# Values and z projected with tokens stationary, a running minimum in the softmax, and the forgetting mask as a matmul

## The chip, the cores and the metric

The kernel runs on one core of one Trainium2 chip. A core has five engines that run side by side: TensorE (PE, with its weight loads shown apart as PEld), VectorE (DVE), ScalarE (ACT), GpSimd (POOL) and SyncE (SP), which here only issues DMA transfers. The metric is device time in microseconds (us) of one execution.

## The reference

One decoder layer on x of 2048 tokens by 1024 channels: an RMS norm, one wide input projection, three causal attention branches that read it, a SiLU gate z on each branch, a branch projection with a sigmoid gate, an output projection, a residual and a last RMS norm. Cut to what matters here:

```python
h = rmsnorm(x, norm_g[l]);  proj = h @ w_in[l]
# diff (4 heads of 128): two softmaxes with a linear bias, pd = p0 - lam * p1, o = pd @ v
# fox  (8 heads of 64):  s = q.k * scale + c[q] - c[k];  s = where(causal, s, -inf);  p = softmax(s);  o = p @ v
# dil  (8 heads of 64):  three banded patterns, each with its row max m, denominator and numerator, merged by exp(m - mx)
y = branch_out * silu(z)
```

## The kernel before

All projections use numbers split in two float16 halves, a high and a low one, so a product takes three matmuls (high.high, high.low, low.high) for each of the 8 blocks of 128 input channels: 24 matmuls that accumulate in one PSUM bank. The normalised input lies transposed on chip, channels on partitions, as `xT[half][token quarter]`, each 128 x 8 x 512.

The work runs as 12 groups, four of each branch (g0 to g3 diff, g4 to g7 fox, g8 to g11 dil). Each group has 128 channels of q and k for two heads (u = 0, 1), 128 of v and 128 of z, and some of the 24 merge-gate projections ride along. `drive` emits a group's attention as jobs; between their steps, the `Filler` emits pieces of projection work (v, then the next group's q and k, z, gates) by a credit in estimated nanoseconds: each generator step yields its estimate, and `pump` runs steps until the credit is spent. The order that then stands on each engine is made by a scheduler from this program order, from the dependencies and from the number of buffers in each pool.

A q/k, v, z or gate unit (`mm_steps`, line 385) takes 512 tokens: the 128 x 128 weight block is stationary and 512 columns of `xT` stream past, so the result has channels on partitions. That suits q and k. Values and z must have tokens on partitions. So `fill_v` and `z_unit` evict the bank as two float16 halves (ACT line 544 or 572, DVE line 545 or 573) and send them through a DMA transpose on SP's queue (line 546 or 574); for z, POOL then adds the two transposed halves (line 575). Dil groups also write v to DRAM and read it back in strides (lines 549, 1038, 1040).

A softmax row block (`softmax_rows`, 128 queries) runs over its keys in chunks of 512: two matmuls make the scores (`scores`, lines 661 and 662, tile `s_g`), and one DVE instruction (line 696, `CUSTOM_DVE_ANT_0`) adds the bias, writes the sum to an `e` tile and takes the row maximum of the chunk, which a second small instruction, `DVE_READ_ACCUMULATOR2_ANT`, puts into a column of `pm`. In fox, the last chunk is read in two such instructions: the block on the diagonal takes its bias from `bl`, a copy of the bias that POOL has masked (line 964), the rest takes `R`. Then a reduction over the columns (line 703) and a multiplication by minus the score scale (line 704, or 706 for one column) give `nm`, and ACT takes exp(c * e + nm) (line 710). The dil jobs do the same by blocks (lines 1109, 1112, 1114, 1118). After that, `e` is split in two float16 halves (ACT 727, DVE 728), transposed by DMA into `eT` (line 736, tile pool of 6), and multiplied with v on PE (lines 718, 721, tile `po_g`). The `e` tiles are a pool of 5 and become free when their transposes have landed; the score banks are 3 and become free when line 696 or 1109 has read them.

Of the kernel before, what the change touches and what calls it, by code (L numbers as in the profile page):

```python
# [19 lines left out]
P = 128  # L20
# [136 lines left out]
def tile_hybrid_trunk(  # L157
# [27 lines left out]
    make_identity(nc, ident)  # L185

# [341 lines left out]

    def fill_v(gr):
        if gr["br"] == 2:  # L530
            gr["vd"] = dr.tile([S, 2, P], F16, tag="vd", name=f"vd_{gr['n']}", bufs=2)
        wt = w_need(("v", gr["g"]))
        for t4 in range(4):
            pd = dn_bank(f"pv_{gr['n']}_{t4}")
            prs = []
            for k in range(KC):
                wh, wl = wsl(wt, 0, k), wsl(wt, 1, k)
# [22 lines left out]
    def z_unit(gr, t4):  # L560
        wt = w_need(("z", gr["g"]))
        z = gr["z"]
        pd = dn_bank(f"pz_{gr['n']}_{t4}")
        prs = []
        for k in range(KC):
            wh, wl = wsl(wt, 0, k), wsl(wt, 1, k)
            prs += [(wh, xT[0][t4][:, k]), (wh, xT[1][t4][:, k]), (wl, xT[0][t4][:, k])]
        yield from mm_steps(pd, prs, 216, 6)
        hl = gs_tile(f"zs_{gr['n']}_{t4}").bitcast(F16)
        zt = gs_tile(f"zt_{gr['n']}_{t4}").bitcast(F16).rearrange("p (b c) -> p b c", b=8)  # L570
# [88 lines left out]
    def scores(gr, u, q2s, qsl, ps, ksl):  # L659
# [12 lines left out]
    def softmax_rows(gr, u, q2, qb, bias_of, diag, den_of, name):  # L672
        n = qb + 1
        nk = n * P
        nch = (n + 3) // 4
        qsl = slice(P * qb, P * qb + P)
        off = P * (qb % 4)
        pm = st1("pm", f"pm_{name}", 5)
        np_ = 0
        et = []  # L680
        for ch in range(nch):
            w = min(512, nk - 512 * ch)
            if ch % 2 == 0:
                et.append(e_tile(f"e_{name}_{ch // 2}", (P, 1280)))
                live[0] += 1
            ps = sc_bank(f"s_{name}_{ch}")
            scores(gr, u, q2[:, off:off + P], qsl, ps[:, :w], slice(512 * ch, 512 * ch + w))
            o = 256 + 512 * (ch % 2)
            segs = [(0, w, bias_of(512 * ch, w))]
            if diag is not None and ch == nch - 1:  # L690
                segs = [(w - P, P, diag)]
                if w > P:
                    segs.append((0, w - P, bias_of(512 * ch, w - P)))
            for a, sw, b in segs:
                with hp(H_TT):
                    rd = V.tensor_tensor_reduce(out=et[ch // 2][:, o + a:o + a + sw], in0=ps[:, a:a + sw], in1=b, scale=1.0, scalar=-3e38,  # L696
                                           op0=ALU.add, op1=ALU.max, accum_out=pm[:, np_:np_ + 1])
                np_ += 1
            reads.append(rd)
            yield  # L700
        nm = st1("nm", f"nm_{name}")
        if np_ > 1:
            V.tensor_reduce(nm, pm[:, :np_], axis=AX.X, op=ALU.max)
            V.tensor_mul(nm, nm, gr["nc"][u])  # L704
        else:
            V.tensor_mul(nm, pm[:, 0:1], gr["nc"][u])
# [66 lines left out]
    def jobs_diff(gr):  # L773
# [7 lines left out]
        def job(qb):  # L781
# [5 lines left out]
            def S_():  # L787
# [6 lines left out]
                for u in range(2):  # L794
                    et = yield from softmax_rows(
                        gr, u, q2[u], qb, lambda a, w: bias[:, S - P - P * qb + a:S - P - P * qb + a + w], None,
# [6 lines left out]
                V.tensor_mul(a, den[:, 0, 0:1], nlam)  # L803
                V.tensor_mul(a, a, rO[:, qb, 1:2])
# [142 lines left out]
    def jobs_fox(gr):  # L947
# [6 lines left out]
        def job(u, qb):  # L954
# [4 lines left out]
            def S_():  # L959
                R = gr["R"][u]  # L960
                if qb % 4 == 0:
                    q2[u] = make_q2(gr, u, qb // 4)
                bl = bl_tile(f"bl_{name}")
                G.affine_select(out=bl, in_=R[:, P * qb:P * qb + P], pattern=[[-1, P]], compare_op=ALU.is_ge, fill=NEG,
                                base=0, channel_multiplier=1)
                hold["e"] = yield from softmax_rows(
                    gr, u, q2[u], qb, lambda a, w: R[:, a:a + w], bl,
# [75 lines left out]
    def jobs_dil(gr):  # L1043
# [17 lines left out]
        def job(p, bs):  # L1061
# [11 lines left out]
            def S_():  # L1073
# [3 lines left out]
                for h in range(0, len(bs), 2):  # L1077
# [5 lines left out]
                    nm = st1("nm2", f"nm_{name}_{h}", 4, 8)  # L1083
                    for a, b in enumerate(bs[h:h + 2]):
# [15 lines left out]
                        for u in range(2):  # L1100
                            cut = p == 0 and w > P and j % 4 == 0
                            am = st1("amx", f"amx_{name}_{b}_{u}", 2) if cut else None
                            for c in range(1 + cut):
# [62 lines left out]
    def post_dil(gr):  # L1166
# [511 lines left out]
```

## Time and profile before

| | |
|---|---|
| median of 3 runs (lowest, highest) | 2784.61 us (2780.58, 2785.28) |
| the profiled execution's own time | 2802.34 us |
| its span, first to last instruction | 2800.6 us |
| PE / DVE / ACT / POOL busy | 2634.3 / 2088.7 / 1669.5 / 383.4 us |
| mean granted TensorE clock | 0.932 |

The profile is of one execution, and its own time is 17.7 us (0.6%) above the median of the three timed runs. The span leaves 1.7 us of its time outside. Busy times are sums over instructions; PE's are modelled at their ends, so that a chain of short gaps can hide in a busy PE. The groups follow each other in time: diff from about 100 to 900 us, fox to 1650 us, dil to 2400 us, and then the branch and output projections.

### The profile page before, as it was taken

Reading aid. Unit: us, or ns where it says so; the run is one execution under the profiler, and the core shown is the slowest. Engines: PE = TensorE matmul, PEld = TensorE weight load, DVE = VectorE, ACT = ScalarE, POOL = GpSimd, SP = SyncE. Lnnn points to the kernel's source line nnn. Section 1 sums busy time; section 2 is a strip of 40 time slices with the busy share of each in tenths; the row PEclk is TensorE's granted clock in tenths of the full one; section 3 lists DMA queues with packets and bytes.
Section 4 is the critical chain, followed back from the end, with each engine's and each line's share of the span. In section 5 each row is a group of like instructions: output and inputs, shape, how many; then the busy total and the mean of one; then the engine's idle time right before and its main releaser. Section 6 shows DMA issues by size and latency. Waiting matters only on the chain.

```text
span 2800.6 us, 48432 instructions
## 1 busy us (share of the span) xinstructions
PE 2634.3 (94%) x16264; PEld 1378.4 (49%) x16264; DVE 2088.7 (75%) x7120; ACT 1669.5 (60%) x3642; POOL 383.4 (14%) x565
## 2 busy tenths in 40 slices
PE   7999999999999999999999998998979887999998
PEld 4455445455455444454455444544545444444555
DVE  8687978977977868778778776667667665678855
ACT  6466666656566666666676656756758577435311
POOL 0000200200102102102111120132041310400000
PEclk9899999989999999999999999998989998999999
DMA  4345445444455787887886878679687799764222
GB/s 159 74 88 111 89 92 108 99 83 110 90 105 112 140 162 143 159 156 148 150 167 131 153 137 145 133 149 162 138 158 156 139 204 230 212 187 137 95 100 76
DMA packets 981834, 377.02 MB, mean 135 GB/s; under 512 B 842824, under 2 KB 939856, under 8 KB 980048
## 3 DMA queue, kind: packets, MB, share of 16 engines
q1 hardware_dynamic: 981584, 373.93, 63.3%
q8 instruction: 127, 2.08, 0.3%
q14 instruction: 123, 1.01, 0.1%
HBM read 118.14 MB, written 59.05 MB: 63 GB/s over the span
## 4 chain that ended last, share of the span: by engine, by line
PE 58%; DVE 13%; DMA 12%; ACT 8%; issue 5%; SPq 2%; POOL 1%; DVEq 0%; ACTq 0%; POOLq 0%
PE pq_g L385 12%; PE pg L385 11%; PE pbr L385 9%; DMA eT_g<-e_g 6%; PE pz_g L385 5%; PE pout L1485 4%; PE po_g L718 3%; PE pv_g L385 3%; PE s_g L661 3%; PE s_g L662 3%; ACT e_g L1118 2%; DVE e_g L728 2%; PE pout L1486 2%; DVE e_g L696 2%; PE po_g L721 2%
## 5 line engine op out<-in xcount | busy, mean ns | idle before, releaser
L385 PE MATMUL pg<-xT,w_g 128*128 128x512 f16 x2304 | 582.9, 394 | 4.4 <-ACT gs L593 2.8
L710 ACT ACTIVATE e_g<-e_g,nm_g,c_g 128x1024 f32<-128x1024 f32 (+7 forms) x384 | 377.6, 984 | 251.4 <-DVE nm_g L704 218.4
L385 PE MATMUL pq_g<-xT,w_q 128*128 128x512 f16 x1536 | 388.4, 399 | 15.5 <-DVE stk_g L416 14.8
L728 DVE SCALAR_TENSOR_TENSOR e_g<-e_g 128x512 f16<-128x512 f32 (+2 forms) x480 | 316.4, 669 | 89.0 <-ACT e_g L727 86.4
L718 PE MATMUL po_g<-v_g,eT_g 128*128 128x128 f16 (+1 forms) x2232 | 315.4, 236 | 34.6 <-DMA eT_g<-e_g 16.8
L385 PEld LDWEIGHTS <-w_g 128*128 128x128 f16 x2304 | 223.6, 101 | 244.3 <-issue 13.9
L727 ACT ACTIVATE e_g<-e_g 128x512 f16<-128x512 f32 (+2 forms) x480 | 265.9, 569 | 91.3 <-DVE e_g L728 86.7
L385 PE MATMUL pz_g<-xT,w_z 128*128 128x512 f16 x1152 | 288.4, 390 | 6.5 <-DVE stk_g L416 5.3
L721 PE MATMUL po_g<-v_g,eT_g 128*128 128x64 f16 (+1 forms) x2232 | 293.6, 201 | 0.0
L385 PE MATMUL pv_g<-xT,w_v 128*128 128x512 f16 x1152 | 283.2, 395 | 2.8 <-DVE vs_g L545 1.4
L1118 ACT ACTIVATE e_g<-e_g,nm_g,c_g 128x256 f32<-128x256 f32 (+1 forms) x384 | 207.8, 543 | 111.0 <-DVE nm_g L1114 109.0
L385 PE MATMUL pbr<-u,w_b 128*128 128x512 f16 x1152 | 264.9, 393 | 4.1 <-ACT gs L593 1.9
L718 PEld LDWEIGHTS <-eT_g 128*128 128x128 f16 x2232 | 211.2, 100 | 87.0 <-DMA eT_g<-e_g 25.2
L661 PE MATMUL s_g<-stk_g 128*128 128x512 f16 (+3 forms) x640 | 228.1, 358 | 25.1 <-DVE pm_g L696 24.7
L721 PEld LDWEIGHTS <-eT_g 128*128 128x128 f16 x2232 | 206.5, 99 | 78.7 <-issue 21.7
L385 PEld LDWEIGHTS <-w_q 128*128 128x128 f16 x1536 | 148.7, 102 | 178.1 <-DVE stk_g L416 16.7
L696 DVE CUSTOM_DVE_ANT_0 e_g<-s_g,bias_g 128x512 f32<-128x512 f32 (+3 forms) x320 | 190.3, 605 | 60.8 <-DMA eT_g<-e_g 39.1
L662 PE MATMUL s_g<-stk_g,q_g 128*128 128x512 f16 (+3 forms) x640 | 229.0, 360 | 0.2 <-issue 0.2
L696 DVE CUSTOM_DVE_ANT_0 e_g<-s_g,R_g 128x512 f32<-128x512 f32 (+3 forms) x288 | 171.5, 597 | 43.9 <-DMA eT_g<-e_g 29.7
L385 PEld LDWEIGHTS <-w_b 128*128 128x128 f16 x1152 | 115.3, 100 | 146.6 <-issue 8.1
L385 PEld LDWEIGHTS <-w_v 128*128 128x128 f16 x1152 | 114.8, 101 | 134.9 <-issue 7.9
L1485 PE MATMUL pout<-wo,acc 128*128 128x512 f16 x512 | 172.7, 389 | 0.0
(476 smaller groups left out, 4331.7 us busy)
## 6 DMA issues: line engine op xcount, KB each, us to landing
gd<-gs SPq DMA_DIRECT2D x96, 256.0 KB, 2.7
gt<-gd SPq DMA_DIRECT2D x24, 1024.0 KB, 5.2
w_g<-in_w_in_dram SPq DMA_DIRECT2D x24, 512.0 KB, 4.1
ud<-y_g SPq DMA_DIRECT2D x48, 256.0 KB, 3.1
eT_g<-e_g SPq DMA_TRANSPOSE x640, 3.2
od_g<-ro_g SPq DMA_DIRECT2D x64, 132.0 KB, 2.3
xb<-in_x_dram SPq DMA_DIRECT2D x16, 512.0 KB, 6.5
q_g<-stk_g SPq DMA_DIRECT2D x128, 64.0 KB, 2.3
```

Source lines behind the costliest of these rows:

```text
L385: T.matmul(dst, l, r, start=(i == 0), stop=(i == n - 1))
L661: behind_read(T.matmul(ps, stk[:, 0, qsl], stk[:, 1, ksl], start=True, stop=False))
L662: T.matmul(ps, q2s, stk[:, 1, ksl], start=False, stop=True)
L696: rd = V.tensor_tensor_reduce(out=et[ch // 2][:, o + a:o + a + sw], in0=ps[:, a:a + sw], in1=b, scale=1.0, scalar=-3e38, op0=ALU.add, op1= ...
L710: A.activation(e[:, 256:256 + w], e[:, 256:256 + w], AF.Exp, bias=nm, scale=gr["c"][u], accum_out=den_of(i))
L718: ins = T.matmul(po, eh, vv, start=first, stop=False)
L721: T.matmul(po[:, 0], el, vv[:, 0], start=False, stop=last)
L727: A.activation(h[:, :w], f, AF.Copy, scale=scale)
L728: V.scalar_tensor_tensor(h[:, w:], f, scale, h[:, :w], op0=ALU.mult, op1=ALU.subtract)
L1118: A.activation(eu, eu, AF.Exp, bias=nm[:, 2 * a + u:2 * a + u + 1], scale=gr["c"][u], accum_out=sm[:, a, 2 + u:3 + u])
L1485: T.matmul(po, ah, wo[un][k], start=k == 0, stop=False)
L1486: T.matmul(po[:, 0], al, wo[un][k][:, 0], start=False, stop=k == KC - 1)
```

## The change

There are three parts.

1. Values and z: `mm_tokens` makes 128 tokens (a slice of `xT`) stationary and streams the 128 columns of the weight block, for four token blocks side by side in one bank. The result has tokens on partitions. So v is evicted straight into its two halves, z straight into float32 by one ACT instruction, and the 96 DMA transposes, z's low half on DVE and z's sum on POOL are gone. A unit has 96 matmuls of 128 columns in place of 24 of 512.
2. Softmax: the DVE instruction multiplies by the negative score scale itself (a scalar read from a tile) and takes a minimum that starts from the value of the chunk before (another such scalar). The last chunk's result is `nm` as exp needs it; the reduction and the multiplication are gone, and exp has the constant scale -1. Dil keeps scaled minima too, down to `post_dil`.
3. Forgetting mask: a third matmul, of the constants `cut` (identity and triangle, bfloat16), adds the mask to the diagonal block's scores in PSUM. POOL's masked copy `bl` and the second DVE instruction of the last chunk are gone.

```diff
+    cut = cp.tile([P, 2, P], BF16, name="cut")
+    V.tensor_copy(cut[:, 0], ident)
+    G.memset(cut[:, 1], 0.0)
+    G.affine_select(out=cut[:, 1], in_=cut[:, 1], pattern=[[-1, P]], compare_op=ALU.is_ge, fill=NEG, base=0, channel_multiplier=1)
...
+    def mm_tokens(pd, wt, t4):
+        for b in range(4):
+            prs = []
+            for k in range(KC):
+                wh, wl = wsl(wt, 0, k), wsl(wt, 1, k)
+                xh, xl = (xT[a][t4][:, k, P * b:P * b + P] for a in range(2))
+                prs += [(xh, wh), (xh, wl), (xl, wh)]
+            yield from mm_steps(pd[:, P * b:P * b + P], prs, 56, 12)
...
     def fill_v(gr):
...
-                prs += [(wh, xT[0][t4][:, k]), (wh, xT[1][t4][:, k]), (wl, xT[0][t4][:, k])]
-            yield from mm_steps(pd, prs, 216, 6)
-            hl = gs_tile(f"vs_{gr['n']}_{t4}").bitcast(F16)
+            yield from mm_tokens(pd, wt, t4)
...
-                A.activation(hl[:, :512], pd, AF.Copy, scale=QSH)
-                V.scalar_tensor_tensor(hl[:, 512:], pd, QSH, hl[:, :512], op0=ALU.mult, op1=ALU.subtract)
-                Q.dma_start_transpose(vt, hl)
+                pb = pd.rearrange("p (b c) -> p b c", b=4)
+                A.activation(vt[:, 0:4], pb, AF.Copy, scale=QSH)
+                V.scalar_tensor_tensor(vt[:, 4:8], pb, QSH, vt[:, 0:4], op0=ALU.mult, op1=ALU.subtract)
...
     def z_unit
...
-            A.activation(hl[:, :512], pd, AF.Copy, scale=QSH)
-            V.scalar_tensor_tensor(hl[:, 512:], pd, QSH, hl[:, :512], op0=ALU.mult, op1=ALU.subtract)
-            Q.dma_start_transpose(zt, hl)
-        G.tensor_tensor(z[:, 4 * t4:4 * t4 + 4], zt[:, 0:4], zt[:, 4:8], op=ALU.add)
+            A.activation(z[:, 4 * t4:4 * t4 + 4], pd.rearrange("p (b c) -> p b c", b=4), AF.Copy, scale=QSH)
...
     def scores
         behind_read(T.matmul(ps, stk[:, 0, qsl], stk[:, 1, ksl], start=True, stop=False))
+        if diag:
+            T.matmul(ps[:, ps.shape[1] - P:], cut[:, 0], cut[:, 1], start=False, stop=False)
         T.matmul(ps, q2s, stk[:, 1, ksl], start=False, stop=True)
...
     def softmax_rows
...
-            segs = [(0, w, bias_of(512 * ch, w))]
-            if diag is not None and ch == nch - 1:
-                segs = [(w - P, P, diag)]
-                if w > P:
-                    segs.append((0, w - P, bias_of(512 * ch, w - P)))
-            for a, sw, b in segs:
...
-                    rd = V.tensor_tensor_reduce(out=et[ch // 2][:, o + a:o + a + sw], in0=ps[:, a:a + sw], in1=b, scale=1.0, scalar=-3e38,
-                                           op0=ALU.add, op1=ALU.max, accum_out=pm[:, np_:np_ + 1])
+                rd = V.tensor_tensor_reduce(out=et[ch // 2][:, o:o + w], in0=ps[:, :w], in1=bias_of(512 * ch, w), scale=gr["nc"][u], scalar=nm,
+                                       op0=ALU.add, op1=ALU.min, accum_out=mn_)
+            nm = mn_
...
-            V.tensor_reduce(nm, pm[:, :np_], axis=AX.X, op=ALU.max)
-            V.tensor_mul(nm, nm, gr["nc"][u])
...
-                A.activation(e[:, 256:256 + w], e[:, 256:256 + w], AF.Exp, bias=nm, scale=gr["c"][u], accum_out=den_of(i))
+                A.activation(e[:, 256:256 + w], e[:, 256:256 + w], AF.Exp, bias=nm, scale=-1.0, accum_out=den_of(i))
...
     jobs_diff
-                V.tensor_mul(a, den[:, 0, 0:1], nlam)
-                V.tensor_mul(a, a, rO[:, qb, 1:2])
+                V.scalar_tensor_tensor(a, den[:, 0, 0:1], nlam, rO[:, qb, 1:2], op0=ALU.mult, op1=ALU.mult)
...
     jobs_fox
-                bl = bl_tile(f"bl_{name}")
-                G.affine_select(out=bl, in_=R[:, P * qb:P * qb + P], pattern=[[-1, P]], compare_op=ALU.is_ge, fill=NEG,
-                                base=0, channel_multiplier=1)
...
     jobs_dil
-                                    rd = V.tensor_tensor_reduce(out=eo, in0=pi, in1=bi, scale=1.0, scalar=-3e38, op0=ALU.add, op1=ALU.max,
-                                                           accum_out=am[:, c:c + 1] if cut else sm[:, a, u:u + 1])
-                            if cut:
-                                V.tensor_max(sm[:, a, u:u + 1], am[:, 0:1], am[:, 1:2])
+                                    rd = V.tensor_tensor_reduce(out=eo, in0=pi, in1=bi, scale=gr["nc"][u], scalar=am if c else 3e38, op0=ALU.add, op1=ALU.min,
+                                                           accum_out=am if c < cut else sm[:, a, u:u + 1])
...
-                        V.tensor_mul(nm[:, 2 * a:2 * a + 2], sm[:, a, 0:2], gr["nc2"])
```

On PE, at the start of fox group g5's v unit (`pv_g5_0` is its bank, `w_v_5` its weights, `xT0` and `xT1` the input's halves), there stood before:

```order
L385 LDWEIGHTS w_v_5_11820
L385 MATMUL pv_g5_0_12690<-xT0_0_88,w_v_5_11820 128x512
L385 LDWEIGHTS w_v_5_11820
L385 MATMUL pv_g5_0_12690<-xT1_0_92,w_v_5_11820 128x512
L385 LDWEIGHTS w_v_5_11820
L385 MATMUL pv_g5_0_12690<-xT0_0_88,w_v_5_11820 128x512
```

And now there stands, in the same place:

```order
L389 LDWEIGHTS xT0_0_94
L389 MATMUL pv_g5_0_15043<-w_v_5_14229,xT0_0_94 128x128
L389 LDWEIGHTS xT0_0_94
L389 MATMUL pv_g5_0_15043<-w_v_5_14229,xT0_0_94 128x128
L389 LDWEIGHTS xT1_0_98
L389 MATMUL pv_g5_0_15043<-w_v_5_14229,xT1_0_98 128x128
```

The stationary operand is now the input and the stream is a quarter as long; each matmul still has a weight load of its own, so PE has four pairs where it had one.

On SP, at the start of dil group g8, there stood before (`vs_g8` are v's evicted halves, `eT_g8` transposed scores, `ud1` the store of group g7's output):

```order
L549 DMA vd_g8_20567<-v_g8_1_20740 128x4x128 x2
L1038 DMA v1_g8_20905<-vd_g8_20567 128x1x1024
L736 DMA_TRANSPOSE eT_g8_0_2_0_20755<-e_g8_0_2_20586 128x8x128
L546 DMA_TRANSPOSE v_g8_2_20810<-vs_g8_2_20809 128x8x128
L1231 DMA ud1_75<-y_g7_17885 128x1024 x3
L549 DMA vd_g8_20567<-v_g8_2_20810 128x4x128 x2
L1231 DMA ud1_75<-y_g7_17885 128x1024
L736 DMA_TRANSPOSE eT_g8_0_2_1_20759<-e_g8_0_2_20586 128x8x128
```

And now:

```order
L725 DMA_TRANSPOSE eT_g8_0_2_0_24390<-e_g8_0_2_24103 128x8x128
L725 DMA_TRANSPOSE eT_g8_0_2_1_24394<-e_g8_0_2_24103 128x8x128
L557 DMA vd_g8_24067<-v_g8_1_24370 128x4x128 x2
L725 DMA_TRANSPOSE eT_g8_0_4_0_24550<-e_g8_0_4_24147 128x8x128
L725 DMA_TRANSPOSE eT_g8_0_4_1_24554<-e_g8_0_4_24147 128x8x128
L1023 DMA v1_g8_24678<-vd_g8_24067 128x1x1024
```

The two transposes of one `e` tile now stand together, with no transpose of v and no store of g7 between them.

On DVE, around the end of fox row block 9 of g5 (three chunks; `nm` is exp's bias, `c_g5` the scales), there stood before:

```order
L696 ISA e_g5_0_9_1_13146,pm_g5_0_9_13088<-s_g5_0_9_2_13147,bl_g5_0_9_13084 128x128
L696 ISA pm_g5_0_9_13088 128x1
L696 ISA e_g5_0_9_1_13146,pm_g5_0_9_13088<-s_g5_0_9_2_13147,R_g5_0_12661 128x128
L696 ISA pm_g5_0_9_13088 128x1
...
L703 TENSOR_REDUCE nm_g5_0_9_13197<-pm_g5_0_9_13088 128x1
...
L704 TENSOR_TENSOR nm_g5_0_9_13197<-nm_g5_0_9_13197,c_g5_9902 128x1
```

And now:

```order
L691 ISA e_g5_0_9_0_15669,nm_g5_0_9_1_15718<-s_g5_0_9_1_15715,R_g5_0_15017,nm_g5_0_9_0_15673,c_g5_11882 128x512
L691 ISA nm_g5_0_9_1_15718 128x1
...
L691 ISA e_g5_0_9_1_15720,nm_g5_0_9_2_15725<-s_g5_0_9_2_15721,R_g5_0_15017,nm_g5_0_9_1_15718,c_g5_11882 128x256
L691 ISA nm_g5_0_9_2_15725 128x1
```

The last chunk is one instruction, it reads the chunk before's `nm`, and its own `nm` is the one exp waits for: before, two more instructions with others between them came first.

## Rows read from the trace of the kernel before

**Rows 1.** Head of the page: span, then each engine's busy time, share, instructions.

```profile
span 2800.6 us, 48432 instructions
PE 2634.3 (94%) x16264; PEld 1378.4 (49%) x16264; DVE 2088.7 (75%) x7120; ACT 1669.5 (60%) x3642; POOL 383.4 (14%) x565
```

**Rows 2.** The page's chain of waits, by engine.

```profile
PE 58%; DVE 13%; DMA 12%; ACT 8%; issue 5%; SPq 2%; POOL 1%; DVEq 0%; ACTq 0%; POOLq 0%
```

**Rows 3.** Stretches: length; PE, PEld, DVE, ACT, POOL busy; clock, DMA share, GB/s.

```profile
100.00:900.00 800.00, 777.47 (x4532) 400.69 (x4530) 654.05 (x2125) 492.38 (x980) 75.46 (x68) 0.93 0.48 99
900.00:1650.00 750.00, 715.15 (x4926) 371.17 (x4925) 584.48 (x2042) 495.38 (x1011) 115.06 (x186) 0.94 0.78 150
1650.00:2400.00 750.00, 663.20 (x4383) 359.32 (x4382) 504.89 (x1991) 497.02 (x1319) 162.98 (x269) 0.91 0.80 160
2400.00:2800.00 400.00, 392.90 (x2009) 200.68 (x2007) 276.25 (x719) 126.85 (x225) 25.05 (x34) 0.94 0.43 134
```

**Rows 4.** Waits of PE: who waited for whom, us in total, times, longest.

```profile
PE s_g L661 <- DVE pm_g L696: 24.7, 33, 2.3
PE s_g L1095 <- DVE amx_g L1109: 20.8, 4, 6.7
```

**Rows 5.** Timeline of SP at 1699 to 1709 us: start, duration, instruction.

```profile
1699.07 3.99 SPq L546 DMA_TRANSPOSE v_g<-vs_g  x1
1703.11 2.38 SPq L1231 DMA_DIRECT2D ud<-y_g  x3
...
1708.19 1.28 SPq L736 DMA_TRANSPOSE eT_g<-e_g  x1
```

**Rows 6.** Timeline of DVE, then of PE, just after; idle before in brackets.

```profile
1711.54 0.29 DVE L1109 CUSTOM_DVE_ANT_0 e_g<-s_g,bd_g 128x128 f32<-128x128 f32 x1 [9.60 <-DMA eT_g<-e_g]
...
1712.53 0.40 PE L1095 MATMUL s_g<-stk_g 128*128 128x256 f16 x1 [6.73 <-DVE amx_g L1109]
```

**Rows 7.** Timeline of PE: a run of 75 matmuls of 512 columns.

```profile
2503.25 17.03 PE L385 MATMUL pbr<-u,w_b 128*128 128x512 f16 x75
```

**Rows 8.** Timeline of PE: scores of 128 columns, the first and the last of nine.

```profile
1689.05 0.22 PE L1095 MATMUL s_g<-stk_g 128*128 128x128 f16 x1
...
1689.50 0.28 PE L1095 MATMUL s_g<-stk_g 128*128 128x256 f16 x1
```

**Rows 9.** Timeline of PE: 120 forget-gate matmuls of 8 columns, tokens stationary.

```profile
581.66 3.20 PE L385 MATMUL pf<-fw,xT 128*128 128x8 f16 x120
584.72 0.59 PE L661 MATMUL s_g<-stk_g 128*128 128x512 f16 x1
```

**Rows 10.** Groups by line on DVE: busy, mean ns | idle before it.

```profile
L704 DVE TENSOR_TENSOR nm_g<-nm_g,c_g 128x1 f32<-128x1 f32 x216 | 36.5, 171 | 2.5
L703 DVE TENSOR_REDUCE nm_g<-pm_g 128x1 f32<-128x2 f32 (+3 forms) x216 | 32.1, 150 | 1.9
L1114 DVE TENSOR_TENSOR nm_g<-sm_g,c_g 128x2 f32<-128x2 f32 x128 | 20.9, 172 | 0.7
L1114 DVE TENSOR_TENSOR nm_g<-s_g,c_g 128x2 f32<-128x2 f32 x64 | 17.6, 289 | 0.2
```

**Rows 11.** Groups on DVE, each shape apart.

```profile
L696 DVE CUSTOM_DVE_ANT_0 e_g<-s_g,bias_g 128x512 f32<-128x512 f32 x224 | 151.8, 685 | 46.1 <-DMA eT_g<-e_g 29.7 <-PE s_g L662 12.4 <-PE po_g L721 2.7
L696 DVE CUSTOM_DVE_ANT_0 e_g<-s_g,bl_g 128x128 f32<-128x128 f32 x128 | 36.4, 286 | 25.9 <-DMA eT_g<-e_g 22.5 <-PE pz_g L385 2.7 <-PE s_g L662 0.4
L573 DVE SCALAR_TENSOR_TENSOR zs_g<-pz_g,zs_g 128x512 f16<-128x512 f32 x48 | 32.8, 684 | 7.1 <-ACT zs_g L572 6.7
L657 DVE SCALAR_TENSOR_TENSOR xT<-px,gx,xT 128x512 f16<-128x512 f32 x32 | 23.3, 746 | 3.7 <-ACT xT L656 3.5
```

**Rows 12.** Instructions that write z's transposed tile: ns min/median/max, first and last.

```profile
L574 SPq DMA_TRANSPOSE zt_g<-zs_g x48: 1231/1260/2747, 176.7 to 2347.8; - x48
```

**Rows 13.** Timeline of DVE: three small instructions, one after the other.

```profile
1203.54 0.15 DVE L306 TENSOR_REDUCE am_q<-amp_q 128x1 f32<-128x2 f32 x1
1203.65 0.16 DVE L703 TENSOR_REDUCE nm_g<-pm_g 128x1 f32<-128x3 f32 x1
1203.85 0.16 DVE L704 TENSOR_TENSOR nm_g<-nm_g,c_g 128x1 f32<-128x1 f32 x1
```

More of the change, by code (lines that the diff above doesn't have):

```diff
@@ L534, in fill_v @@
             pd = dn_bank(f"pv_{gr['n']}_{t4}")
-            prs = []
-            for k in range(KC):
-                wh, wl = wsl(wt, 0, k), wsl(wt, 1, k)
-                prs += [(wh, xT[0][t4][:, k]), (wh, xT[1][t4][:, k]), (wl, xT[0][t4][:, k])]
-            yield from mm_steps(pd, prs, 216, 6)
-            hl = gs_tile(f"vs_{gr['n']}_{t4}").bitcast(F16)
+            yield from mm_tokens(pd, wt, t4)
             vt = v_tile(f"v_{gr['n']}_{t4}", (P, 8, P))
@@ L563, in z_unit @@
         pd = dn_bank(f"pz_{gr['n']}_{t4}")
[L564 to L570, printed above, removed]
+        yield from mm_tokens(pd, wt, t4)
         with hp(H_EV):
-            A.activation(hl[:, :512], pd, AF.Copy, scale=QSH)
-            V.scalar_tensor_tensor(hl[:, 512:], pd, QSH, hl[:, :512], op0=ALU.mult, op1=ALU.subtract)
-            Q.dma_start_transpose(zt, hl)
-        G.tensor_tensor(z[:, 4 * t4:4 * t4 + 4], zt[:, 0:4], zt[:, 4:8], op=ALU.add)
+            A.activation(z[:, 4 * t4:4 * t4 + 4], pd.rearrange("p (b c) -> p b c", b=4), AF.Copy, scale=QSH)
     def fill_z(gr):
@@ L657, in x_phase, with scores @@
             V.scalar_tensor_tensor(xT[1][tg][:, k], pt, gx[:, k:k + 1], hi, op0=ALU.mult, op1=ALU.subtract)
-    def scores(gr, u, q2s, qsl, ps, ksl):
+    def scores(gr, u, q2s, qsl, ps, ksl, diag):
         stk = gr["stk"][u]
         behind_read(T.matmul(ps, stk[:, 0, qsl], stk[:, 1, ksl], start=True, stop=False))
+        if diag:
+            T.matmul(ps[:, ps.shape[1] - P:], cut[:, 0], cut[:, 1], start=False, stop=False)
         T.matmul(ps, q2s, stk[:, 1, ksl], start=False, stop=True)
@@ L677, in softmax_rows @@
         off = P * (qb % 4)
-        pm = st1("pm", f"pm_{name}", 5)
-        np_ = 0
+        nm = 3e38
         et = []
@@ L686, in softmax_rows @@
             ps = sc_bank(f"s_{name}_{ch}")
-            scores(gr, u, q2[:, off:off + P], qsl, ps[:, :w], slice(512 * ch, 512 * ch + w))
+            scores(gr, u, q2[:, off:off + P], qsl, ps[:, :w], slice(512 * ch, 512 * ch + w), diag and ch == nch - 1)
             o = 256 + 512 * (ch % 2)
-            segs = [(0, w, bias_of(512 * ch, w))]
-            if diag is not None and ch == nch - 1:
-                segs = [(w - P, P, diag)]
-                if w > P:
-                    segs.append((0, w - P, bias_of(512 * ch, w - P)))
-            for a, sw, b in segs:
-                with hp(H_TT):
-                    rd = V.tensor_tensor_reduce(out=et[ch // 2][:, o + a:o + a + sw], in0=ps[:, a:a + sw], in1=b, scale=1.0, scalar=-3e38,
-                                           op0=ALU.add, op1=ALU.max, accum_out=pm[:, np_:np_ + 1])
-                np_ += 1
+            with hp(H_TT):
+                mn_ = st1("nm", f"nm_{name}_{ch}", 1, 12)
+                rd = V.tensor_tensor_reduce(out=et[ch // 2][:, o:o + w], in0=ps[:, :w], in1=bias_of(512 * ch, w), scale=gr["nc"][u], scalar=nm,
+                                       op0=ALU.add, op1=ALU.min, accum_out=mn_)
+            nm = mn_
             reads.append(rd)
             yield
-        nm = st1("nm", f"nm_{name}")
-        if np_ > 1:
-            V.tensor_reduce(nm, pm[:, :np_], axis=AX.X, op=ALU.max)
-            V.tensor_mul(nm, nm, gr["nc"][u])
-        else:
-            V.tensor_mul(nm, pm[:, 0:1], gr["nc"][u])
         for i, e in enumerate(et):
@@ L1101, in S_ @@
                             cut = p == 0 and w > P and j % 4 == 0
-                            am = st1("amx", f"amx_{name}_{b}_{u}", 2) if cut else None
+                            am = st1("amx", f"amx_{name}_{b}_{u}") if cut else None
                             for c in range(1 + cut):
@@ L1174, in post_dil @@
         w = st.tile([P, 3, NB, 2], F32, tag="wc", name=f"wc_{n}", bufs=1)
-        V.tensor_max(mx, s1[:, :, 0:2], sp[:, 0, :, 0:2])
-        V.tensor_max(mx, mx, sp[:, 1, :, 0:2])
+        V.tensor_tensor(mx, s1[:, :, 0:2], sp[:, 0, :, 0:2], op=ALU.min)
+        V.tensor_tensor(mx, mx, sp[:, 1, :, 0:2], op=ALU.min)
         for p in range(3):
             V.tensor_sub(w[:, p], sts[p][:, :, 0:2], mx)
-        for u in range(2):
-            A.activation(w[:, :, :, u], w[:, :, :, u], AF.Exp, scale=gr["c"][u])
+        A.activation(w, w, AF.Exp, scale=-1.0)
         for p in range(3):
```

7 lines of the change are left out of this document (3 added, 4 removed).

## Prediction

> **What bounds the kernel now.** I read the head of the page first. PE is busy 2634.3 of 2800.6 us, DVE 2088.7, ACT 1669.5 [rows 1]; the reader is to see that one engine is nearly full and that a second is not far off. The chain of waits agrees: PE holds 58% of it, DVE and DMA 13% and 12% [rows 2]. So there are two ways to gain: less work on PE, or fewer of the moments at which PE stands still. The view by stretches says how large those moments are. In the diff, fox and dil stages PE is idle for 800 - 777.5 = 22.5, 34.9 and 86.8 us, together 144 [rows 3]. Its clock reads 0.95 where nothing is lost, and 0.93, 0.94 and 0.91 over these stages, which at 0.95 for full speed is another 17 + 8 + 32 = 57 us [rows 3]. So about 200 us can be had from stalls, half of them in dil, and none in the last 400 us of projections, where PE is busy 392.9 of 400.
>
> What ends the stalls: PE waits for score banks that DVE has not read yet, in all attention branches; the two largest rows of PE's waits say so [rows 4]. In dil, DVE itself had been idle, since the `e` tiles come free only when their transposes have landed. At 1699 to 1712 us the chain can be seen whole: SP spends 3.99 us on one transpose of v, 2.38 us on three stores behind it, and issues the transpose of scores at 1708.19 [rows 5]; DVE was idle for 9.60 us until that `e` tile was free, and PE for 6.73 us until DVE had read a bank [rows 6].
>
> **Part 1, values and z with tokens stationary.** On PE, 96 units (12 groups, v and z, 4 quarters) lose 24 matmuls of 512 columns each, 2304 in all, and gain 96 of 128, 9216 in all. The columns are the same, so the question is whether a quarter as long a matmul costs a quarter. 75 matmuls of 512 take 17.03 us; less about 0.4 for the last one's own run, that is 224.7 ns from start to start [rows 7]. Nine score matmuls of 128 columns, each with a weight load of its own, start within 1689.50 - 1689.05 = 0.45 us, 56.3 ns apart [rows 8]. Four of these are 225.0 ns, so the sum is 2304 x 0.3 ns = 1 us. The rows are read to 10 ns, so 55.0 to 57.5 ns is open, which is -11 to +12 us. Could the weight loads not keep up? 120 pairs of load and matmul with 8 columns, tokens stationary from the same input tiles, start 3.06 us / 120 = 25.5 ns apart [rows 9]. So a load needs less than half of the 56 ns, and 240 instructions in a row were delivered at twice the rate that is now asked for.
>
> Here the Trainium skill speaks against the change. Its page "TensorE: Matmul & The Clock Gate", section "Wait — 56ns, not 53.3ns?", says that each matmul pays about 2.5 ns beside its columns, however many there are. Cutting one into four would then cost 7.5 ns, 2304 x 7.5 = 17 us, and the result would be some 16 us later than mine. The trace does not show such a fixed part: 224.7 against 4 x 56.3 ns.
>
> Beside PE, this part takes 96 DMA transposes off SP's queue, at a median 1.26 us of issue [rows 12], 121 us of SP; v's four per group stood among the transposes of scores. DVE loses z's 48 low halves, 32.8 us [rows 11]. ACT has the same number of evictions, and POOL, busy 383 of 2800 us, loses sums that nobody on the chain waited for: nothing either way. The eviction of z now writes the z tile itself, where POOL wrote it later. If that tile were still held by the group before, ACT would stall with everything queued behind it, exps above all; but z comes in the second part of a group's fill, after the post-processing that frees the tile, so I cost it at nothing.
>
> **Part 2, the running minimum.** On DVE it removes 216 reductions, 32.1 us, 216 multiplications, 36.5 us, and dil's 192, 20.9 + 17.6 us [rows 10]. A further 128 one-column instructions go (40 rows with one chunk, 64 in diff's `a`, 24 dil maxima), at line 704's 171 ns 22 us. It adds scalars read from a tile to 1048 instructions (640 chunks, 408 in dil). No row shows this instruction with such a scalar. The nearest pair is z's low half, with a constant, at 684 ns, and the same operation on the same shape from PSUM with a scalar from a tile, at 746 [rows 11]: 62 ns. I take that: 1048 x 62 = 65 us. Bounds: nothing, if the read hides behind the accumulator's; and at the other end 62 more for the second scalar in the 408 that continue a minimum (25 us), plus the wait for it. That wait is bounded by a reduction and the multiplication that reads it, 0.20 us from start to start, against 0.11 for two that do not depend on each other [rows 13]: 408 x 0.09 = 37 us. Others stand between the chunks in most places, so I take none of it. What also goes is delay: exp no longer waits for two instructions and what was queued between them.
>
> **Part 3, the mask by a matmul.** 128 matmuls of 128 columns, 128 x 56.3 ns = 7 us of PE, all of it on the path. DVE reads the last chunk once instead of twice in 96 of the 128 row blocks. A piece of 128 columns takes 286 ns and one of 512 takes 685 [rows 11], so a column costs 1.04 ns and the fixed part of a piece is 153 ns: 96 x 153 = 15 us. POOL's masked copies were off the chain.
>
> **The sum.** DVE: 32.8 + 32.1 + 36.5 + 38.5 + 22 + 15 = 177 us removed, 65 added, 112 less, of the 1743 it is busy in the three stages [rows 3], 6%; by the bounds 50 to 177. PE: +1 + 7 = +8 us, sure as far as the pitch is. The stalls: in dil, where v's 16 transposes stood before those of the scores, I let half of them give back 3 us each, less than the 3.99 seen [rows 5], 24 us. Of the other 175 us I let DVE's shorter queue return a tenth, somewhat more than its 6%, since a queue near 80% gives more than its share: 16 us. That is 40 us of 200, and what is late next is still the transposes of the scores, of which not one goes. Bounds: nothing, and twice that. Sum: +8 - 40 = -32 us. The profiled execution took 2802.3 us, so 2770 for it; its excess over the median, 17.7 us, I take as common to both, so the forecast is 2784.6 - 32 = 2753 us, 1.1% faster.
>
> **The rivals.**
> A. *Twice the return.* DVE's relief and SP's come together, since every stall runs through both (`e` tile, score bank). For: half of the idle time is in dil, where one transpose of v lay ahead of a 9.60 us wait [rows 6]. Against: the scores' own transposes stay, and the DMA share there is 0.80 [rows 3]. 80 us back: 2784.6 + 8 - 80 = 2713 us.
> B. *The scalars eat DVE's relief.* The dearer bound: 65 + 25 + 37 = 127 of the 177 us are spent again. Then only SP's relief counts, 24 us, and a few us of DVE's: 2784.6 + 8 - 24 - 4 = 2765; if half of SP's gain also turns into waits for the remaining transposes, 2778. Against: most DVE time is not on the chain [rows 2].
> C. *Slower: 128 columns do not hold 56 ns.* The trace shows such streams only for nine matmuls at a time, and a unit now has 96. If the pitch were 61 ns, 9216 x 4.7 = 43 us more on an engine that is 94% busy: 2796 with my full return, 2816 with half of it. It decides from 3.5 ns on, 32 us / 9216. Against: the 120 pairs at 25.5 ns [rows 9].
> The fixed cost that the skill states would be a third of the way there, 2769.
> D. *It does not do what it says.* The stalls have fixed places where a group begins, and a later wait takes the place of each; the time is then 2784.6 + 8 less some 5 us, 2788.
>
> **How the numbers follow.** My forecast with its own range, 2735 to 2770, has 0.48. A has 0.17, B 0.14, C 0.12, D 0.09. Differences under 0.2%, 5.6 us, are about what a measurement of this kernel cannot tell from no change. Faster than 2779 are my forecast, A, and three quarters of B: 0.76 with a little of C. Within 0.2% are the rest of B and two thirds of D: 0.11. Slower are C and the rest of D: 0.13. The range reaches over A's centre below and to C's point above: 2708 to 2796 us.
>
> **What would show it.** In the profile after: the rows of v and z with 9216 matmuls, a run of which starts every 56 to 57 ns (C if 60); PE's idle time in dil at 86.8 - 24 us or less (A if 50), and the clock there above 0.91; DVE busy near 1980 us, with the chunk instruction at about 685 + 62 ns (B if over 800, or if DVE waits for itself). I am wrong if PE's idle time stays near 144 us in the three stages, or if the projections of v and z hold PE longer than before.

## The result, and the profile after

The changed kernel takes 2752.08 us (2748.17 to 2755.53, four runs), the kernel before in the same session 2784.95; the ratio is 0.9886, 95% interval 0.9872 to 0.9901. The forecast was 2753. A second timing (run `c4_after`) gave 0.9887 (0.9871 to 0.9903).

The time is as forecast, yet two terms of the sum were wrong and nearly cancelled. To see it, one trap has to be cleared first. In the profile of before, TensorE's granted clock reads 0.95 of 2.4 GHz even where PE never stops (the longer stretches of [rows 3] read 0.91 to 0.94). In every later profile, of either kernel, it reads 1.00 there. One such stretch, in the profiles of before and after (columns as in [rows 3]; the clock is the third figure from the end):

```profile
2480.00:2520.00 40.00, 40.00 (x181) 17.93 (x179) 28.93 (x84) 11.67 (x21) 0.00 (x0) 0.95 0.63 180
2480.00:2520.00 40.00, 40.00 (x189) 18.42 (x187) 33.32 (x98) 19.41 (x32) 0.00 (x0) 1.00 0.57 164
```

So the first profile is not subtracted from the profile after; a later profile of the unchanged kernel is (run `c0_before`). Its head, answering to [rows 1]:

```profile
span 2769.9 us, 48432 instructions
...
PE 2559.3 (92%) x16264; PEld 1357.0 (49%) x16264; DVE 2085.8 (75%) x7120; ACT 1666.9 (60%) x3642; POOL 384.2 (14%) x565
```

and that of the changed kernel:

```profile
span 2746.5 us, 61047 instructions
...
PE 2565.5 (93%) x23304; PEld 1660.5 (60%) x23304; DVE 2043.8 (74%) x6129; ACT 1620.1 (59%) x3642; POOL 281.8 (10%) x391
```

PE has 7040 matmuls more and is busy 6 us longer in a span 23 us shorter (busy time also holds short gaps, since the ends of matmuls are modelled). DVE's busy time falls by 42 us, not by 112. The stretches of [rows 3], of the unchanged kernel and then of the changed one (same columns; the last now ends at 2740):

```profile
100.00:900.00 800.00, 759.34 (x4550) 395.39 (x4550) 655.40 (x2128) 492.92 (x981) 81.07 (x73) 0.98 0.48 99
900.00:1650.00 750.00, 700.05 (x4978) 368.08 (x4977) 592.40 (x2059) 502.14 (x1027) 118.35 (x190) 0.99 0.79 151
1650.00:2400.00 750.00, 652.99 (x4374) 357.34 (x4372) 503.67 (x1987) 497.48 (x1319) 165.90 (x276) 0.95 0.80 162
2400.00:2740.00 340.00, 340.00 (x1801) 176.44 (x1800) 247.96 (x644) 109.95 (x191) 12.82 (x17) 1.00 0.46 142
```

```profile
100.00:900.00 800.00, 753.36 (x6883) 497.05 (x6882) 634.41 (x1776) 473.71 (x968) 55.84 (x49) 0.97 0.42 87
900.00:1650.00 750.00, 714.12 (x7349) 471.56 (x7347) 576.55 (x1641) 495.40 (x1035) 52.12 (x51) 1.00 0.74 142
1650.00:2400.00 750.00, 676.50 (x6827) 467.38 (x6826) 509.11 (x1786) 481.27 (x1332) 164.41 (x275) 0.96 0.78 158
2400.00:2740.00 340.00, 337.85 (x1822) 178.37 (x1820) 250.87 (x666) 109.75 (x193) 3.68 (x4) 1.00 0.41 130
```

PE's idle time: diff 40.7 to 46.6 us, fox 49.9 to 35.9, dil 97.0 to 73.5. Dil and fox gain, diff loses a little.

What PE's own work costs is read from its timeline. A run of 67 matmuls of v (128 columns) and what follows it, then a run of 24 of 512 columns and what follows:

```profile
300.61 3.90 PE L389 MATMUL pv_g<-w_v,xT 128*128 128x128 f16 x67
304.35 0.38 PE L660 MATMUL s_g<-stk_g 128*128 128x512 f16 x1
...
2449.66 5.34 PE L389 MATMUL pbr<-u,w_b 128*128 128x512 f16 x24
2454.84 0.27 PE L211 MATMUL pb_b<-ident,am_b 128*128 128x128 f32 x1
```

3.74 us / 67 = 55.8 ns; 5.18 us / 24 = 215.8 ns. Four short ones cost 223.3 ns, 7.5 more than one long one: 2304 x 7.5 = 17 us, where the forecast had 1. With the mask's 7 us, PE has 24 us more to do, not 8. At these prices, and those of the other widths read in the same way, I counted the matmuls of each stage (from the first v matmul of its first group to that of the next stage, in dil to the last matmul that writes `po_g`) and call the rest of its time lost, idle or at the lower clock:

| us | before: length, lost | after: length, lost |
|---|---|---|
| diff | 766.6, 55.6 | 783.3, 63.4 |
| fox | 787.3, 74.3 | 770.7, 49.1 |
| dil | 703.6, 128.5 | 685.0, 95.7 |
| whole execution | lost 288.8 | lost 242.4 |

A second profile of the changed kernel (`c4_after`) has stages of 777.4, 773.9 and 690.2 us. So one profile fixes a stage only to some 6 us, and smaller differences are not read below.

The stalls give back 46 us by this pair of profiles, where the forecast had 40. (The medians are 33 us apart, the two profiled executions 23, since each lies a few us from its median; by the medians the stalls' return is 33 + 24 = 57.)

DVE's chunk instruction in the changed kernel, answering to [rows 11]: with its bias, the scale (`c_g`) and, from the second chunk on, the minimum so far (`nm_g`) instead of a constant:

```profile
L691 DVE CUSTOM_DVE_ANT_0 e_g<-s_g,bias_g,nm_g 128x512 f32<-128x512 f32 x120 | 96.8, 806 | 27.3 <-DMA eT_g<-e_g 13.2 <-PE s_g L663 12.0
...
L1093 DVE CUSTOM_DVE_ANT_0 e_g<-s_g,bd_g,c_g 128x256 f32<-128x256 f32 x192 | 84.8, 479 | 25.5 <-PE s_g L1082 21.3 <-DMA eT_g<-e_g 3.6
...
L691 DVE CUSTOM_DVE_ANT_0 e_g<-s_g,R_g,c_g 128x512 f32<-128x512 f32 x104 | 77.6, 746 | 9.0 <-PE s_g L663 5.8 <-PE pz_g L389 2.2 <-DMA eT_g<-e_g 0.7
```

685 ns became 746 with one scalar from a tile and 806 with two. The waits of PE now, answering to [rows 4] (on the rows of `pb_g` and `pb_z`, PE is to transpose the maxima of a weight block that DVE has not finished):

```profile
PE s_g L660 <- DVE nm_g L691: 52.6, 45, 3.0
PE pb_g L211 <- DVE am_g L310: 30.3, 5, 10.5
PE pb_z L211 <- DVE am_z L310: 14.6, 1, 14.6
```

The second and third are new among the largest: 45 us in six waits. The first shows one in dil on SP, DVE and PE:

```profile
1880.62 1.23 SPq L1025 DMA_DIRECT2D v_g<-vd_g  x1
1881.89 1.14 SPq L328 DMA_DIRECT2D w_g<-in_w_in_dram  x1
```

```profile
1893.00 1.28 DVE L308 TENSOR_REDUCE amp_g<-w_g 128x1 f32<-128x512 f32 x2 [12.64 <-DMA w_g<-in_w_in_dram]
```

```profile
1897.58 0.47 PE L211 MATMUL pb_g<-ident,am_g 128*128 128x128 f32 x1 [10.54 <-DVE am_g L310]
```

The load of a weight block is issued right behind the strided re-reads of v, and DVE can begin its maxima only 11.1 us later. The reading of scores is queued behind them, and PE stands still. The four largest of the six waits, 41 us, are of this kind, one in each dil group; in two of them only three of the five re-reads stand ahead of the load.

### The profile page after: what moved, and what is told of

It reads as the page before. It is cut to its first block, busy times and chain, and to the rows that moved or that the text cites. A ratio compares the mean times of both kernels' runs of the same rounds, so it can differ in the third digit from the quotient of the medians.

```text
span 2746.5 us, 61047 instructions
## 1 busy us (share of the span) xinstructions
PE 2565.5 (93%) x23304; PEld 1660.5 (60%) x23304; DVE 2043.8 (74%) x6129; ACT 1620.1 (59%) x3642; POOL 281.8 (10%) x391
## 5 line engine op out<-in xcount | busy, mean ns | idle before, releaser
L389 PEld LDWEIGHTS <-xT 128*128 128x128 f16 x9600 | 562.6, 99 | 38.7 <-issue 8.7
L389 PE MATMUL pg<-xT,w_g 128*128 128x512 f16 x2304 | 555.8, 380 | 0.3 <-ACT xT L655 0.3
L699 ACT ACTIVATE e_g<-e_g,nm_g 128x1024 f32<-128x1024 f32 (+7 forms) x384 | 342.9, 893 | 220.6 <-DVE nm_g L691 206.4
L389 PE MATMUL pq_g<-xT,w_q 128*128 128x512 f16 x1536 | 373.4, 385 | 2.7 <-DVE stk_g L420 2.4
L389 PE MATMUL pz_g<-w_z,xT 128*128 128x128 f16 x4608 | 297.8, 221 | 3.2 <-ACT z_g L574 2.7
L389 PE MATMUL pv_g<-w_v,xT 128*128 128x128 f16 x4608 | 294.3, 222 | 1.1 <-ACT w_v L320 1.1
L389 PE MATMUL pbr<-u,w_b 128*128 128x512 f16 x1152 | 254.5, 380 | 3.9 <-ACT z_g L574 1.5
L710 PEld LDWEIGHTS <-eT_g 128*128 128x128 f16 x2232 | 203.8, 99 | 51.6 <-issue 7.2
L716 ACT ACTIVATE e_g<-e_g,lamA 128x512 f16<-128x512 f32 (+3 forms) x160 | 103.3, 656 | 115.2 <-DVE e_g L796 74.3
L1093 DVE CUSTOM_DVE_ANT_0 e_g<-s_g,bd_g,c_g 128x256 f32<-128x256 f32 (+1 forms) x384 | 142.3, 413 | 38.3 <-PE s_g L1082 33.1
L691 DVE CUSTOM_DVE_ANT_0 e_g<-s_g,bias_g,nm_g 128x512 f32<-128x512 f32 (+3 forms) x192 | 135.5, 706 | 40.2 <-DMA eT_g<-e_g 20.5
```

Source lines behind the costliest of these rows:

```text
L389: T.matmul(dst, l, r, start=(i == 0), stop=(i == n - 1))
L691: rd = V.tensor_tensor_reduce(out=et[ch // 2][:, o:o + w], in0=ps[:, :w], in1=bias_of(512 * ch, w), scale=gr["nc"][u], scalar=nm, op0=ALU. ...
L710: T.matmul(po[:, 0], el, vv[:, 0], start=False, stop=last)
L716: A.activation(h[:, :w], f, AF.Copy, scale=scale)
L1093: rd = V.tensor_tensor_reduce(out=eo, in0=pi, in1=bi, scale=gr["nc"][u], scalar=am if c else 3e38, op0=ALU.add, op1=ALU.min, accum_out=am ...
```

## The experiments

Each was timed in five rounds against the kernel before on the same chip. `lost` is the column of the table above.

**The kernel before, unchanged** (no edit). Is the difference of the two first profiles one of clock?

> The kernel before, unchanged, for its clock. In the first profile PE's clock at full speed read 0.95 (512 columns every 224.7 ns); in the changed kernel's it read 1.00 (every 216 ns), in code that both share too. Theory S (the gain comes from fewer stalls): the level belongs to the execution, not to the kernel; here the clock may read 1.00, the time is 1.000 of before within 0.2%, and idle plus half-clock time of PE, counted at the same level, is 30 to 50 us more than in the changed kernel. Rival K (the gain is the clock: something that the change took away or thinned out holds the level at 0.95): here it reads 0.95 again, in every run, mean 0.93, and the stalls are no longer than in the changed kernel.

Ratio 0.9996 (0.9986 to 1.0005), 2772.8 us, clock 1.00 in the projections, as in the profile after, and stalls 46 us longer than there, as theory S said. The mean clock of all 42 timed executions of this kernel in the session is 0.974 to 0.980, against 0.932 in the first profile. So the level does not belong to the kernel, and the gain is not one of clock. What set it to 0.95 in the one execution is not shown.

**Each part alone.** The line of each that decides:

```diff
+            yield from mm_tokens(pd, wt, t4)                       # part 1: c1_tokens
+                scale=gr["nc"][u], scalar=nm, op0=ALU.add, op1=ALU.min   # part 2: c2_runmin (diagonal still apart)
+            T.matmul(ps[:, ps.shape[1] - P:], cut[:, 0], cut[:, 1], ...)  # part 3: c3_mask
```

> Part 1 alone: values and z with tokens stationary, no transposes of them; softmax and mask as before. Theory S: PE work +1 us, 20 to 30 us of stalls back, most of them in dil: ratio 0.990 to 0.993. Rival K: the level rises to 1.00 with this part alone (the streams of 128 columns are what differs on PE), ratio 0.985 to 0.990, with PE's idle time not smaller. Rival C of the forecast (128 columns dearer than 56 ns): slower, 1.005 or more.

> Part 2 alone: the scaled running minimum (the fox diagonal still as two instructions with POOL's masked copy; they continue the minimum too). Theory S: DVE some 100 us less busy than before, 8 to 16 us of stalls back: ratio 0.994 to 0.997. Rival B of the forecast (the scalars eat DVE's relief): the chunk instruction over 800 ns, ratio 0.998 to 1.003. Rival K: clock and time as before, 0.95 and 1.000.

> Part 3 alone: the forgetting mask by a matmul; the last chunk read by one instruction; maxima, reductions and multiplications as before. Theory S: 7 us more PE work, 15 us less of DVE: ratio 1.000 to 1.003. A theory that DVE in fox is what PE waits for says 0.997 to 1.000. Rival K: 1.002 to 1.003.

Part 1: 0.9990 (0.9980 to 0.9999), lost 270.0, DVE busy 2042.0, 44 less than before. Part 2: 0.9969 (0.9956 to 0.9981), lost 284.8, DVE busy 2112.0, 26 more than before. Part 3: 1.0032 (1.0019 to 1.0045), lost 297.0. Their product is 0.9991: added up alone, the parts are worth nothing, together 1.1%. Part 1 takes 19 us of stalls, a little less than theory S said, and pays 17 on PE. Part 2 was to relieve DVE by 100 us and makes it busier.

**The changed kernel again, parts 1 and 2, parts 2 and 3** (no other edit).

> The changed kernel, unchanged, beside the kernel before on one chip. Alone, the three parts gave 0.999, 0.997 and 1.003. If they add up, the whole gives 0.999; if they need each other (part 1 frees the queue and the e tiles, and only then is DVE what PE waits for), it gives 0.987 to 0.990 as in the first measurement, at the same clock level as before, so that the gain is no matter of the chip.

> Parts 1 and 2 without the mask by a matmul (POOL's masked copy and the two instructions for the fox diagonal are back; the minimum runs over both). If part 3 costs in company what it cost alone, this is 0.3% faster than the whole change: 0.984 to 0.986. If DVE is what PE waits for once part 1 is in, the 96 extra DVE instructions cost more than the 7 us of PE that go: 0.989 to 0.993, and the loss shows in the fox stage alone.

> Parts 2 and 3 together (running minimum scaled in the reading of scores, mask by a matmul), v and z projected as before with their transposes. Alone part 2 gave 0.9969, part 3 1.0032, part 1 0.9990; all three gave 0.9887. Theory 'mask frees the chain' (part 3 makes each last chunk of a fox row one reading instead of two with a minimum handed between them, so parts 2 and 3 need each other and part 1 is worth little): ratio 0.990 to 0.993, VectorE busy 30 to 60 us under part 2 alone. Rival 'three-way' (the room on VectorE is only turned into time where v and z no longer wait for its evictions of transposes): 0.997 to 1.000, about the product of the two, 1.000.

All three: 0.9887, lost 242.0, so the parts need each other. Parts 1 and 2: 0.9933 (0.9917 to 0.9948), lost 254.5; the fox stage is 782.7 us against 773.9 with the mask, and the other two are not longer beyond their scatter, as the theory said in which DVE is what PE waits for. Parts 2 and 3: 1.0023 (1.0010 to 1.0036), lost 296.1, DVE busy 2091.0, 5 us more than before. So parts 2 and 3 take no busy time off DVE, and without part 1 they gain nothing; my theory that the mask frees the chain of minima is refuted, and the rival came nearer, though the run is slower still than it said. Part 1 in company takes 54 us of stalls (296.1 to 242.0) and pays 17 on PE; alone it takes 19. PE's largest waits with parts 2 and 3 alone:

```profile
PE s_g L665 <- DVE nm_g L696: 47.4, 51, 2.5
PE po_g L712 <- DMA eT_g<-e_g: 33.8, 22, 4.2
PE s_g L1084 <- DVE s_g L1098: 30.9, 7, 10.0
```

With part 1 as well, the second is 10.7 us, and scores of dil wait 4.5 us for DVE. For dil that is no meeting of parts: with part 1 alone its scores wait 12.4 us for DVE, where those of the kernel before wait 36.5 (`c1_tokens`, `c0_before`). Where the parts meet is seen in the lengths of the stages, here as changes against the kernel before:

| us | diff | fox | dil |
|---|---|---|---|
| part 1 alone | +27.1 | -11.2 | -11.7 |
| part 2 alone | +10.0 | -8.3 | -2.4 |
| part 3 alone | +0.4 | +14.0 | +1.5 |
| the three added up | +37.5 | -5.5 | -12.6 |
| all three, `c4_after` | +10.8 | -13.4 | -13.4 |
| all three, the profile after | +16.7 | -16.6 | -18.6 |

In dil the parts about add up. Most of what they gain in company is in diff: part 1 alone costs 27 us there, which eats its gains in fox and dil. PE's waits for DVE at the scores of the diff stage, in the kernel before, with part 1 alone and with all three parts, show part of it:

```profile
PE s_g L661 <- DVE pm_g L696: 22.8, 25, 2.8
PE s_g L656 <- DVE pm_g L691: 40.1, 25, 4.0
PE s_g L660 <- DVE nm_g L691: 30.5, 24, 3.0
```

Part 1 alone lengthens them by 17 us, and with the other two parts 10 of these are gone; what makes up the rest is not shown. In fox PE waits 15.8 us for transposed scores before, 15.1 with part 1, 24.3 with part 2, 25.7 with parts 2 and 3, and 10.7 with all three. So what the shorter softmax brings forward is held there by transposes, unless part 1 has taken those of v and z off the queue; that it is the queue is argued from these waits, and v's transposes were not tried apart from z's. Why the mask costs 15 us beside part 2 alone (0.9969 to 1.0023) and gains 13 beside parts 1 and 2 stays open.

**Diff groups with v and z the old way.**

```diff
+        if gr["br"] == 0:
+            yield from fill_v_old(gr)
+            return
...
+        if gr["br"] == 0:
+            yield from z_unit_old(gr, t4)
+            return
```

> The whole change, but the diff groups keep the old way for v and z: channels on partitions, 24 matmuls of 512 columns, and 32 DMA transposes back on the queue. In the diff stage part 1 alone lost 27 us (794 against 767) where fox and dil gained 11 and 12. Theory O (the order: in diff's v and z units the scores stand closer on PE, 55 chunks where 37 stood, so PE meets score banks that DVE has not read yet, and the fill is missing later): the diff stage goes back from 783 to about 765 us, ratio 0.981 to 0.985. Rival T (tokens stationary is worth as much in diff as elsewhere, and the loss there is from something else): 0.990 to 0.994.

0.9919 (0.9905 to 0.9934); diff 778.2 us against 777.4. So beside parts 2 and 3 the new way costs diff no time: theory O is refuted. The 10 us of diff that are left stand with part 2 alone (776.6 against 766.6) and with parts 2 and 3 (777.1), and not with part 3 alone (767.0), so they come with part 2; by what is not shown. The whole is 0.3% slower than the changed kernel, and no stage of this profile shows where.

**Size of the pieces that are handed out between scores.** `mm_tokens` yields after 12 matmuls, 56 ns of credit each.

```diff
-            yield from mm_steps(pd[:, P * b:P * b + P], prs, 56, 12)
+            yield from mm_steps(pd[:, P * b:P * b + P], prs, 36, 24)
```

> The whole change with the same instructions in another order on PE: the credit that a step of the new v and z units is charged is 36 ns a matmul instead of 56, in steps of 24 matmuls instead of 12, so that diff's v units stand among 35 chunks of scores as before, not 55. Theory O: the diff stage comes to 765 to 772 us and the waits of scores for DVE in v units shrink from 27 to under 15 us; ratio 0.982 to 0.986. Rival: the density of the scores does not matter, the stage stays at 783 and the ratio at 0.988 to 0.990. The order changes elsewhere too, which may cost what is won.

0.9919 (0.9905 to 0.9933): fox 756.1 instead of 773.9, diff 771.7 instead of 777.4, but dil 718.9 instead of 690.2. The 18 us of fox and the 29 of dil are clear of the scatter, the 6 of diff are not. Why dil loses is not shown. Then with 36 and 24 in diff and fox only:

```diff
+                prs, *((56, 12) if gr["br"] == 2 else (36, 24)))
```

> The changed kernel, whose token-stationary matmuls of v and z are handed out 24 at a time (36 ns of credit each) in the diff and fox groups and, as the change has them, 12 at a time (56 ns) in the dil groups. In the run that had 36 and 24 everywhere the diff stage took 771.7 us, the fox stage 756.1 and the dil stage 718.9, against 777.4, 773.9 and 690.2 of the changed kernel. Theory 'by stage' (what a stage gains from the size of its pieces is its own): diff about 772, fox about 756, dil about 690, in all about 23 us under the changed kernel, 2720, ratio to the kernel before 0.980. Rival 'carried over' (PE, ACT and DVE hand on a backlog of work, so what fox wins is work put off, and the dil stage pays it): dil 705 or more, ratio 0.987 or more.

0.9829 (0.9812 to 0.9847), 2727.15 us: diff 772.2, fox 753.3, dil 694.4. Dil does not pay for fox, so the gain is the stage's own; the ratio lies between the two theories. PE's waits for DVE at the scores fall to half, 24.8 us in 19 waits from 51.6 in 48, and in fox from 18.5 to 0.7: with larger pieces between them, a score finds its bank read. The edit changes the size of a piece and its credit, and these were not tried apart.

**The weight load ahead of v's re-read** (dil groups).

```diff
             yield from mm_tokens(pd, wt, t4)
+            if gr["br"] == 2 and t4 == 3:
+                w_start()
...
             gr["vdone"] = 4 * t4 + 4
-        w_start()
+        if gr["br"] < 2:
+            w_start()
```

> The changed kernel, whose next weight load in the four dil groups is issued right after the last matmul of v, ahead of the last store of v and of the strided re-reads of v, instead of behind them. In the changed kernel TensorE waits in the dil stage 47 us in all for the weights' maxima on VectorE, which itself waited 13.6 us for a weight load that took 11 us behind 1 MB of re-read. Theory 'queue' (the load is late because it stands behind the re-read): these waits fall to 25 us or less, dil stage 665 to 680 instead of 690, ratio 0.980 to 0.985. Rival 'moved' (the re-read of v or the transposes of probabilities wait instead, or the maxima move ahead as well and wait as long): waits of 40 us or more in the dil stage, in all 0.987 to 0.990.

0.9849 (0.9829 to 0.9869), 2735.93 us; dil 681.4, against 685.0 and 690.2 in the two profiles of the changed kernel. The same place as above, now on SP, then DVE, then PE:

```profile
1863.98 0.53 SPq L328 DMA_DIRECT2D w_g<-in_w_in_dram  x1
```

```profile
1867.98 1.28 DVE L308 TENSOR_REDUCE amp_g<-w_g 128x1 f32<-128x512 f32 x2 [3.31 <-DMA w_g<-in_w_in_dram]
```

```profile
1871.16 0.48 PE L211 MATMUL pb_g<-ident,am_g 128*128 128x128 f32 x1 [3.69 <-DVE am_g L310]
```

DVE begins 4.0 us after the issue of the load instead of 11.1, and PE waits 3.69 us instead of 10.54. In the four dil groups these times were 8.2, 11.1, 9.4 and 14.6 us and are 7.8, 4.0, 4.3 and 4.0; in the first group the load still stands behind three re-reads. Over dil PE's waits are 24.5 us instead of 44.2. The ratio and the waits are just inside what the queue theory named, and the dil stage is 1 us above it; half of the waits remain.

**Both.**

> The last two edits together: pieces of 24 matmuls in diff and fox, 12 in dil, and the weight load of the dil groups ahead of the re-read of v. If both theories hold and add, diff 772, fox 756, dil 665 to 680, ratio 0.971 to 0.978. If what fox wins is paid in dil and the load's wait only moves, 0.986 to 0.990.

0.9792 (0.9775 to 0.9808), 2717.56 us: faster than both kernels. From 0.9887, the two edits alone take 0.0058 and 0.0038, together 0.0095: they add, unlike the parts of the change, if a little short of the range that I gave. Diff 776.5, fox 759.4 and dil 681.2 us.

```profile
span 2721.5 us, 61043 instructions
...
PE 2572.9 (95%) x23304; PEld 1666.3 (61%) x23304; DVE 2053.9 (75%) x6129; ACT 1612.8 (59%) x3642; POOL 282.7 (10%) x391
```

## Why the prediction was right, and which steps were not

- *What bounds the kernel*: right. Stalls around a nearly full PE were what moved.
- *Part 1 on PE, 1 us*: wrong; 17 us, and one of my own signs of being wrong came with it, that v and z hold PE longer than before. The long row was read right, 224.7 ns, but in an execution whose clock read 0.95, where 512 columns alone are 512 / (0.95 x 2.4) = 224.6 ns. It holds no fixed part that could be read off. At 1.00 a long matmul takes 215.8 ns. The short row was too small: [rows 8] are eight matmuls of 128 columns and one of 256. In that trace the 23 unbroken runs of six or more have a median of 57.3 ns (56.0 in `c0_before`); four of these less 224.7 are 4.5 ns, or 10 us. The rule of the Trainium skill that I set aside, "TensorE: Matmul & The Clock Gate", section "Wait — 56ns, not 53.3ns?", is what the runs show: 215.8 and 55.8 ns are 512 and 128 columns at 2.4 GHz and 2.5 ns each. Rival C, a pitch of 60 ns or more, did not come, and the weight loads do keep up.
- *Part 3 on PE, 7 us*: right, 128 matmuls at 56 ns.
- *DVE 112 us shorter*: wrong; 42, and all of it part 1's. The prices stood: 62 ns for a scalar (746 - 684), and 60 for the second in the 408 that continue a minimum, the 25 us that I put only into the bound. What failed is that I added up durations. By the trace, DVE's instructions add up to 2520.7 us before and 2415.4 after, 105 less, but busy time counts overlaps once (it is no sum over instructions, as the section on the time before says), and the small instructions removed lay over their neighbours: those of [rows 13] are 0.15 and 0.16 us long and start 0.11 and 0.20 us apart. Rival B was right on DVE's relief and wrong on the time.
- *Stalls 40 us shorter*: 46 to 57. The first term held: with part 1 alone the stalls of dil, counted as in the table, are 26 us shorter (24 forecast for v's transposes), and with all three parts 28 to 33. The second, 16 us for DVE's shorter queue, had no ground: part 2 alone takes 4 us of stalls while DVE is busier. In its place stand fox, 23 to 25 us shorter with all three parts and 13 with part 1 alone, and diff, 17 us longer with part 1 alone and 1 to 8 with all three. No term of the sum had that the parts need each other.
- *What is late next*: I named the transposes of scores. They fell (DVE's waits for `e` tiles in front of the chunk instructions, 99.3 us in `c0_before`, are 38.2 after). What is late next is the weight load behind v's re-reads, 41 us of PE in dil.
- The errors, +16 on PE and -6 to -17 on the stalls, have opposite signs. That the total came within 1 us is luck. (Rival B's dearer figure, 2778, adds up to 2777; nothing rests on it.)

## What to carry to other kernels

Before two durations of one profile are set against each other, read the granted clock where the engine never stops: at 0.95 the long matmuls read 4% dearer than in every later profile. Parts that are worth nothing alone are compared stage by stage, since a loss in one can hide gains in the others. On an engine with many small instructions, count what goes from start to start, not durations. And when a change frees a queue, look at what is issued behind its largest transfer: here one load in each of four groups, moved ahead of it, was worth a third of the whole change.

## What was not expected of the hardware

- At a granted clock of 0.95, 512 columns took 224.7 ns instead of 215.8 at 1.00 (4% more), and 128 columns 57.3 instead of 56.0 in the median of 23 runs (2% more): the loss is not in proportion to the clock.
- The DVE reading instruction took 59 to 63 ns more for each scalar that it reads from a tile, at three widths: 284, 347 and 406 ns at 128 columns, 417, 479 and 540 at 256, 684, 746 and 806 at 512 (with the first scalar the maximum also became a minimum).
- DVE could use a 512 KB weight load 4.0 to 4.3 us after its issue ahead of the strided re-reads of v, and 7.8 to 14.6 us after it behind three to five of them on the same queue (256 KB each, the last 1 MB).
